# Moving the l2 norms, the convolution tails and the down-weight sums of a two-layer hybrid decoder

## The chip, the cores and the metric

The kernel runs on one core of a Trainium2 chip. The metric is the device time of one execution in microseconds. The time of the kernel before is the median of three runs, 2936.21 us (2934.1 to 2942.85).

## The reference

Two layers, each with a token-mixing and a channel-mixing sub-layer on a stream of 1024 tokens by 1024 features in float32. Mixing projects the normed stream into four head groups: A and B are gated linear recurrences, C is latent attention, D is a gated delta rule. The part of group D that the change touches is this:

```python
qkv = jax.nn.silu(causal_dwconv(jnp.concatenate([q, k, v], axis=-1), conv_w))   # width 4
qd = l2_norm(heads(qkv[..., :HD * DK_D], HD, DK_D)) * DK_D ** -0.5
kd = l2_norm(heads(qkv[..., HD * DK_D:2 * HD * DK_D], HD, DK_D))
vd = heads(qkv[..., 2 * HD * DK_D:], HD, DV_D)
```

Channel mixing is a gated MLP with D_FF = 2816 and a causal convolution of width 3 on the gate:

```python
gate = causal_dwconv(h @ w_gate, conv_w)
return (jax.nn.gelu(gate, approximate=True) * (h @ w_up)) @ w_down
```

## The kernel before, in words

Products of the projections and of the FFN are exact to about float32: each operand is split into a rounded part (hi, a cast on ScalarE, L197) and a rest (lo, a subtraction on GpSimd or VectorE, L198), and three matmuls (L209, `mm3`) replace one. The code gives a program order. A compile-time scheduler places each instruction in the queue of its engine by that order and by when it takes the operands to be ready, so a queue can hold instructions out of program order; each engine and the DMA queue of SP then work strictly in the order of their queue. `order`, `after` and `issue_after` (`behind` in `ffn1`) add edges that hold an instruction behind another one of the same engine.

**Mixing** (`mixing`, L1068 on) runs `proj_d`, `group_d`, two token-major projections (`tm_copy`), a gate, `proj_c`, `proj_a`, `proj_b`, two gates. One projection tile (`proj_fm`) is a 512 KB weight load through SP into one of two "wst" buffers, a cast on ScalarE, a subtraction on GpSimd, and 48 matmuls of 128x512. In `proj_d` (L809 on) six tiles q, k, v follow each other; each is convolved on VectorE (L825, L827), passed through a silu (L830, L831), and for the first four the squares (L834) are summed over a head by two matmuls with a block matrix of ones (L215), then Ln, Exp and a product on VectorE (L839 to L841) give the norm. All of this stands in the program behind its own tile and ahead of the next tile's projection. Tiles "t" (NT1 = 5 buffers) hold raw values, squares and most other temporaries; tiles "d" (ND = 11) hold q, k, v and group D's matrices.

**Sums of weights.** The FFN uses a Strassen-like scheme: of each pair of tiles seven products take the place of eight. Four of the seven need sums of weight blocks. `down_sums` (L1538) is a generator of 14 steps per layer: 10 pairs of the down weights (to a DRAM tensor `td`) and 4 tiles of the gate/up weights (to `te`). A step loads two tiles of 512 KB (L1550), makes four subtractions on GpSimd (L1555) and stores both tiles (L1562). `next(self.sums)` runs one step at each of 14 places in `mixing`: six in `proj_d`, two after the token-major copies, three in `proj_c`, two in `proj_a`, one of two in `proj_b`.

**FFN1** (`ffn1`, L1239) works through `seq`: 28 early products of the tiles f = 0 to 3 (operands partly from `te`), then seven products per f for f = 4 to 21. `prep(j)` makes the weight operand of product j: loads, sums (`operand_b`, L1223, GpSimd), split. It is called NLA = 7 products ahead; eight "wr" buffers hold operands. From f = 4 on the split of products 0 and 2 is on GpSimd, that of the other five on VectorE. `conv` (L1324) puts the two halves' boundary columns in place (L1329, L1334, GpSimd copies of 128x2), multiplies (L1335 ScalarE, L1337 VectorE twice), and applies the GELU (L1338). `store` (L1340) writes gated tiles and their sums to DRAM through SP. FFN2 (`Back`, `ffn2`) reads `td`.

Of the kernel before, what the change touches and what calls it, by code (L numbers as in the profile page):

```python
# [8 lines left out]
F32 = mybir.dt.float32  # L9
# [14 lines left out]
EPS = 1e-6  # L24
# [104 lines left out]
class Body:  # L129
# [447 lines left out]
    def proj_a(self, l, hT):  # L577
# [27 lines left out]
        for i in range(2):  # L605
            T = self.pt()
            self.proj_fm(l, hT, (AF0 + i, lambda n, p: nc.scalar.activation(
                out=T[:, n * 512:(n + 1) * 512], in_=p, func=AF.Tanh, scale=0.5)))
            next(self.sums, None)
            k = self.pt()  # L610
# [24 lines left out]
    def proj_b(self, l, hT, misc):  # L635
        nc = self.nc
        pp = self.pp
        q = self.pt()
        k = self.pt()
        for m, t in ((BQ, q), (BK, k)):  # L640
            self.proj_fm(l, hT, (m, self.copy_half(t)))
            next(self.sums, None)
        wgk = self.t("p1", "wgk", 1, [16, 128])
        nc.sync.dma_start(out=wgk, in_=self.I["wgk"][l])
        bg = pp[:, PP_BGK:PP_BGK + 1]
        f = self.pt()
        m = self.pt()
        for n in range(2):
            sl = slice(n * 512, (n + 1) * 512)
            p = self.ps([128, 512])  # L650
            self.mm(p, wgk, misc[0:16, sl])
            nc.scalar.activation(out=f[:, sl], in_=p, func=AF.Abs, bias=bg)
            nc.vector.tensor_scalar(out=m[:, sl], in0=p, scalar1=bg, scalar2=0.0, op0=ALU.add, op1=ALU.min)

        nc.scalar.activation(out=f, in_=f, func=AF.Tanh, scale=0.5)
        nc.scalar.activation(out=f, in_=f, func=AF.Ln, scale=0.5, bias=self.bias[0.5])
        nc.vector.tensor_tensor(out=m, in0=m, in1=f, op=ALU.add)
        self.cumsum(f, m)
        return self.spill("B", [q, k, f])


    def proj_c(self, l, hT, misc):
# [3 lines left out]
        for m in (CKV, CQ0, CQ1):  # L666
            t = self.t("k", "ckv", 1) if m == CKV else self.pt()
            self.proj_fm(l, hT, (m, self.copy_half(t)))
            next(self.sums, None)
            ts.append(t)  # L670
# [138 lines left out]
    def proj_d(self, l, hT, misc):  # L809
# [4 lines left out]
        for h in range(2):  # L814
            nc.gpsimd.memset(ones[64 * h:64 * h + 64, 64 * h:64 * h + 64], 1.0)
        fm = []
        for m in range(6):
            raw = self.pt()
            first = [(MISC, self.copy_half(misc))] if m == 0 else []
            self.proj_fm(l, hT, *first, (DQ0 + m, self.copy_half(raw)))  # L820
            next(self.sums)

# [9 lines left out]
            if m < 4:  # L832
                sq = self.pt()
                nc.scalar.activation(out=sq, in_=c, func=AF.Square)  # L834
                for n in range(2):
                    sl = slice(n * 512, (n + 1) * 512)
                    p = self.ps([128, 512])
                    self.mm(p, ones, sq[:, sl])
                    nc.scalar.activation(out=sq[:, sl], in_=p, func=AF.Ln, bias=self.bias[EPS * 4])  # L839
                nc.scalar.activation(out=sq, in_=sq, func=AF.Exp, scale=-0.5)  # L840
                nc.vector.scalar_tensor_tensor(out=c, in0=c, scalar=0.125 if m < 2 else 1.0, in1=sq, op0=ALU.mult, op1=ALU.mult)  # L841
            fm.append(c)
# [225 lines left out]
    def mixing(self, l, hT, x_src, x_dst):  # L1068
# [4 lines left out]
        misc = self.t("p1", "misc", 1)  # L1073
        self.td, self.sums = self.down_sums(l)
        dx = self.proj_d(l, hT, misc)
        od = self.group_d(l, *dx)
        av = self.spill("Av", self.tm_copy(l, TAI, hT))
        next(self.sums)
        bv = self.spill("Bv", self.tm_copy(l, TBV, hT))
        next(self.sums)  # L1080
        aG = self.gate(l, TAG, hT, self.rbh[:, RB_A:RB_A + 64], False)
# [156 lines left out]

    def ffn1(self, l, h, td, te):  # L1239

# [69 lines left out]
        def prep(j):  # L1310
# [5 lines left out]
            else:  # L1316
                if f not in B:
                    fetch(f)
                src = self.operand_b(i, *B[f])
            w = self.t(*(("w", "wr", 4) if j < 4 or j % 2 else ("f1" if j % 8 < 4 else "f0", "wr", 2)), [128, 2, 512], F32R)  # L1320
            self.split(w[:, 0, :], w[:, 1, :], src, nc.vector if j >= n_early and i not in (0, 2) else None)
            W[f, i] = w.rearrange("p e (k f) -> p e k f", f=128)

        def conv(f, n):  # L1324
# [3 lines left out]
            if n:  # L1328
                nc.gpsimd.tensor_copy(out=x[:, 0:2], in_=ends[f] if f < NE else z[f, 0][:, 512:514])  # L1329
            else:  # L1330
                nc.gpsimd.memset(x[:, 0:2], 0.0)
                if f < NE:
                    ends[f] = tails[:, 2 * f:2 * f + 2]
                    nc.gpsimd.tensor_copy(out=ends[f], in_=x[:, 512:514])  # L1334
            nc.scalar.activation(out=c, in_=x[:, 2:514], func=AF.Copy, scale=w(2))  # L1335
# [4 lines left out]
        def store(f):  # L1340

            p, e = divmod(f, 2)
            out = lambda i, x: nc.sync.dma_start(out=gd[7 * p + i], in_=x)
            if p >= NP:
# [30 lines left out]
        tails = self.t("f0", "tails", 1, [128, 2 * NE])  # L1375
        pa, pc, xs = {}, {}, {}
        for j, (f, i) in enumerate(seq):
            if j + NLA < len(seq):
                with behind("s2") if 1 < j < 7 else nullcontext():
                    prep(j + NLA)  # L1380
# [37 lines left out]
            elif i == 6:  # L1418
                add(xs[f, 1], xs[f, 1])
                nc.vector.tensor_tensor(out=g[f, 0], in0=g[f, 0], in1=xs[f, 1], op=ALU.mult)  # L1420
                store(f)
            if (f, i) == (NF - 1, 1):

                back = Back(self, l, gd, td)
                for _ in range(NU):
                    back.prep()
# [106 lines left out]

    def ffn(self, l, h, td, x_src, x_dst, last):
        gd, back = self.ffn1(l, h, *td)
        return self.ffn2(l, back, x_src, x_dst, last)

    def down_sums(self, l):  # L1538


        nc = self.nc
        td = self.dp.tile([NP, 128, 4, 512], F32, tag=self.nm("td"), name=self.nm("td"))
        te = self.dp.tile([NE, 128, 4, 512], F32, tag=self.nm("te"), name=self.nm("te"))

        def steps():
            for p in range(NP + NE):
                w = [self.t("p1", "d", ND) for _ in range(2)]
                for e in range(2):
                    src = self.I["wdn"][l, 2 * p + e] if p < NP else self.I["wgu"][l, p - NP, e].rearrange("p a b -> p (a b)")
                    nc.sync.dma_start(out=w[e], in_=src)  # L1550
                (b11, b12), (b21, b22) = ((x[:, 0:512], x[:, 512:1024]) for x in w)
                if p >= NP:

                    b12, b21 = b21, b12
# [3 lines left out]
                sub(b22, b22, b11)  # L1558
                sub(b21, b21, b22)
                for e in range(2):  # L1560
                    o = td[p] if p < NP else te[p - NP]
                    nc.sync.dma_start(out=o[:, 2 * e:2 * e + 2, :].rearrange("p a b -> p (a b)"), in_=w[e])  # L1562
                yield

        return (td, te), steps()

# [38 lines left out]
    def run(self):  # L1605
# [3 lines left out]
        for l in range(DEPTH):  # L1609
# [4 lines left out]
            dst = self.out if last else self.x2  # L1614
            hT = self.ffn(l, h, self.td, self.x1, dst, last)
            src = dst
# [51 lines left out]

NE, NLA, TRS = 4, 7, (1, 4)

# [32 lines left out]
```

## Time and profile before

| what | before |
|---|---|
| median of three runs | 2936.21 us |
| the profiled execution's own time | 2936.43 us |
| its span, first to last instruction | 2934.6 us |
| TensorE matmul busy | 2736.2 us (93%) |
| VectorE, ScalarE, GpSimd busy | 1838.8, 1328.4, 1187.8 us |
| mean granted TensorE clock | 0.974 |
| DMA | 386 MB, mean 132 GB/s |

The busy line says how much of the span an engine worked. Windows cut the span into stretches, and a stretch in which TensorE is busy for all of its 40 us at full clock can only get faster with less matmul work. Waits say which instruction of another engine or DMA ended an idle stretch. In a timeline a line gives start, duration, engine, line, operation, the tiles written and read, the shape, the number of merged instructions, and in brackets the idle time before and what ended it. SPq is the queue of SP, whose duration of a DMA line includes waiting inside a merged group.

### The profile page before, as it was taken

How to read it: one execution, taken by the hardware profiler on the slowest of the kernel's cores; microseconds unless marked ns; L12 is line 12 of the kernel's file. 1: busy time of each engine (PE TensorE's matmuls, PEld its weight loads, DVE VectorE, ACT ScalarE, POOL GpSimd, SP SyncE). 2: the span in 40 equal slices, each digit the busy share in tenths (PEclk: the TensorE clock that was granted, in tenths of full speed). 3: DMA queues.
4: the chain of work that ended last, by engine and by line, in shares of the span. 5: the costliest groups of instructions: out<-in, count | busy, mean ns of one | idle time of the engine just before them, and what ended most of it. 6: DMA issues, size and time to landing. Idle time of an engine off the chain costs nothing. (4 is left out here: it accounts for less than half of the span.)

```text
span 2934.6 us, 39974 instructions
## 1 busy us (share of the span) xinstructions
PE 2736.2 (93%) x14928; PEld 2224.1 (76%) x14928; DVE 1838.8 (63%) x2658; ACT 1328.4 (45%) x2422; POOL 1187.8 (40%) x1010
## 2 busy tenths in 40 slices
PE   7889888899989999999988998988999999999998
PEld 5688676677768888888767875866777778888887
DVE  4764433896477777665556643338965877776645
ACT  4423334645554444454445233346555544444543
POOL 4522453451675545300155225534526655443001
PEclk9989999999999999999999999999999999999999
DMA  5442553113443233376534315431234433333765
GB/s 188 138 109 66 177 196 113 55 51 111 138 129 112 100 108 108 105 271 195 186 131 149 106 60 197 180 106 58 67 107 144 140 108 101 100 101 104 259 193 194
DMA packets 162674, 386.02 MB, mean 132 GB/s; under 512 B 25488, under 2 KB 37040, under 8 KB 162480
## 3 DMA queue, kind: packets, MB, share of 16 engines
q1 hardware_dynamic: 162480, 383.47, 39.5%
q8 instruction: 117, 1.92, 0.3%
q14 instruction: 77, 0.63, 0.1%
HBM read 273.76 MB, written 109.64 MB: 131 GB/s over the span
## 5 line engine op out<-in xcount | busy, mean ns | idle before, releaser
L209 PE MATMUL pd<-h,wr 128*128 128x512 f32 x2608 | 662.6, 403 | 35.2 <-ACT wr L197 26.6
L209 PEld LDWEIGHTS pd<-h,wr 128*128 128x128 f32 x2608 | 491.1, 191 | 153.9 <-ACT wr L197 28.3
L198 POOL TENSOR_TENSOR wr<-wst,wr 128x512 fp32r<-128x512 f32 (+1 forms) x168 | 307.9, 1837 | 616.1 <-ACT wr L197 606.7
L197 ACT CAST wr<-wst 128x512 fp32r<-128x512 f32 (+1 forms) x260 | 196.6, 759 | 306.8 <-PE pd L209 202.0
L209 PE MATMUL pd<-wr,h 128*128 128x256 f32 x1920 | 249.3, 291 | 0.0
L209 PEld LDWEIGHTS pd<-wr,h 128*128 128x128 f32 x1920 | 242.0, 199 | 1.9 <-issue 0.5
L209 PE MATMUL pm<-h,wr 128*128 128x512 f32 x864 | 230.0, 392 | 1.7 <-DVE x L1399 1.6
L198 DVE TENSOR_TENSOR h<-st,h 128x1024 fp32r<-128x1024 f32 x120 | 152.3, 1272 | 120.9 <-ACT h L197 115.0
L209 PEld LDWEIGHTS pm<-h,wr 128*128 128x128 f32 x864 | 162.0, 188 | 39.3 <-DVE x L1399 2.4
L197 ACT CAST h<-st 128x1024 fp32r<-128x1024 f32 x120 | 125.6, 1049 | 145.8 <-PE pd L209 76.0
L209 PE MATMUL pd<-h 128*128 128x512 f32 x816 | 185.6, 389 | 0.0
L209 PE MATMUL pd<-wr,f 128*128 128x512 f32 x768 | 182.9, 395 | 0.0
L209 PEld LDWEIGHTS pd<-h 128*128 128x128 f32 x816 | 153.2, 188 | 31.8
L1337 DVE SCALAR_TENSOR_TENSOR g<-z,pp,g 128x512 f32<-128x512 f32 x176 | 164.2, 933 | 20.4 <-ACT g L1335 17.9
L209 PEld LDWEIGHTS pd<-wr,f 128*128 128x128 f32 x768 | 142.9, 188 | 32.0 <-ACT f L317 0.9
L209 PE MATMUL pm<-h 128*128 128x512 f32 x720 | 166.1, 391 | 0.7 <-DVE h L198 0.7
L1458 POOL TENSOR_TENSOR y<-y,gb 128x512 f32<-128x512 f32 x24 | 38.3, 1601 | 304.2 <-ACT fc L230 248.3
L198 DVE TENSOR_TENSOR wr<-wst,wr 128x512 fp32r<-128x512 f32 (+1 forms) x92 | 95.9, 1043 | 101.5 <-ACT wr L197 101.5
L209 PEld LDWEIGHTS pm<-h 128*128 128x128 f32 x720 | 135.5, 189 | 29.3 <-DVE h L198 1.1
L215 PE MATMUL pm<-g,g 128*128 128x128 f32 (+1 forms) x672 | 121.2, 329 | 30.1 <-issue 12.9
L215 PEld LDWEIGHTS pm<-g,g 128*128 128x128 f32 x672 | 99.3, 201 | 58.0 <-issue 30.3
L1555 POOL TENSOR_TENSOR d<-d,d 128x512 f32<-128x512 f32 x64 | 109.3, 1708 | 53.5 <-DMA d<-in_wgu_dram 48.3
(364 smaller groups left out, 5483.6 us busy)
## 6 DMA issues: line engine op xcount, KB each, us to landing
st<-gd SPq DMA_DIRECT2D x144, 256.0 KB, 3.0
gd<-g SPq DMA_DIRECT2D x88, 256.0 KB, 2.0
d<-in_wdn_dram SPq DMA_DIRECT2D x40, 512.0 KB, 5.4
td<-d SPq DMA_DIRECT2D x40, 512.0 KB, 2.7
st<-td SPq DMA_DIRECT2D x80, 256.0 KB, 3.6
ust<-in_wgu_dram SPq DMA_DIRECT2D x36, 512.0 KB, 3.7
wst<-in_wgu_dram SPq DMA_DIRECT2D x36, 512.0 KB, 3.6
st<-in_wdn_dram SPq DMA_DIRECT2D x68, 256.0 KB, 3.6
```

Of the source, the lines that this page charges most:

```text
L197: self.marks["hi"] = self.nc.scalar.copy(out=hi, in_=src)
L198: (eng or self.nc.gpsimd).tensor_tensor(out=lo, in0=src, in1=hi.bitcast(F32), op=ALU.subtract)
L209: mm = lambda x, y, **k: self.nc.tensor.matmul(out, lhsT=x, rhs=y, skip_group_check=onto, **k)
L215: self.nc.tensor.matmul(out, lhsT=lhsT, rhs=rhs, start=start, stop=stop)
L1337: nc.vector.scalar_tensor_tensor(out=c, in0=x[:, j:j + 512], scalar=w(j), in1=c, op0=ALU.mult, op1=ALU.add)
L1458: (dve if last and n else pool).tensor_tensor(out=y[t][:, c], in0=y[t][:, c], in1=g_post[:, c], op=ALU.mult)
L1555: sub = lambda o, x, y: nc.gpsimd.tensor_tensor(out=o, in0=x, in1=y, op=ALU.subtract)
```

## The change

- In `proj_d` the matmuls, Ln, Exp and product of the norm of tile m become a function that is called after the projection of tile m + 2.
- `down_sums` becomes `weight_sums`, made twice. In mixing only the four `te` steps are left, all taken from `proj_d`; the store of a step is issued at the next call. The eight later calls in mixing are removed.
- The ten `td` steps of a layer move into FFN1, each in three thirds (loads; subtractions; stores), one third after each product (f, 2) and (f, 6) with f >= 4, behind the last convolution copy on GpSimd and behind the last gated store on SP. They use two buffers "ds".
- To make room, FFN1 has six "wr" buffers in place of eight and NLA is 5 in place of 7. The same early products as before are held behind the split of s2.
- For f < 4 the convolution's boundary copies are on ScalarE in place of GpSimd.

```diff
 proj_d:
-        fm = []
+        fm, norms = [], []
         for m in range(6):
...
             self.proj_fm(l, hT, *first, (DQ0 + m, self.copy_half(raw)))
-            next(self.sums)
+            next(self.sums, None)
+
+            if m > 1:
+                norms.pop(0)()
...
             if m < 4:
                 sq = self.pt()
                 nc.scalar.activation(out=sq, in_=c, func=AF.Square)
-                for n in range(2):
...
+                def norm(c=c, m=m, sq=sq):
+                    for n in range(2):
+                        sl = slice(n * 512, (n + 1) * 512)
+                        p = self.ps([128, 512])
+                        self.mm(p, ones, sq[:, sl])
+                        nc.scalar.activation(out=sq[:, sl], in_=p, func=AF.Ln, bias=self.bias[EPS * 4])
+                    nc.scalar.activation(out=sq, in_=sq, func=AF.Exp, scale=-0.5)
+                    nc.vector.scalar_tensor_tensor(out=c, in0=c, scalar=0.125 if m < 2 else 1.0, in1=sq, op0=ALU.mult, op1=ALU.mult)
+                norms.append(norm)
 mixing (and the next(self.sums) of proj_a, proj_b, proj_c go):
-        self.td, self.sums = self.down_sums(l)
+        self.te, self.sums = self.weight_sums(
+            NE, lambda f, e: self.I["wgu"][l, f, e].rearrange("p a b -> p (a b)"), False, ("p1", "d", ND))
...
-        next(self.sums)
 ffn1, prep:
-            w = self.t(*(("w", "wr", 4) if j < 4 or j % 2 else ("f1" if j % 8 < 4 else "f0", "wr", 2)), [128, 2, 512], F32R)
+            w = self.t(*(("f0", "wr", 2) if j in (4, 5) or j > 5 and j % 3 == 2 else ("w", "wr", 4)), [128, 2, 512], F32R)
 ffn1, conv:
-                nc.gpsimd.tensor_copy(out=x[:, 0:2], in_=ends[f] if f < NE else z[f, 0][:, 512:514])
+                if f < NE:
+                    nc.scalar.copy(out=x[:, 0:2], in_=ends[f])
+                else:
+                    self.marks["conv"] = nc.gpsimd.tensor_copy(out=x[:, 0:2], in_=z[f, 0][:, 512:514])
...
-                    nc.gpsimd.tensor_copy(out=ends[f], in_=x[:, 512:514])
+                    nc.scalar.copy(out=ends[f], in_=x[:, 512:514])
 ffn1, the loop over seq:
+        td, td_steps = self.weight_sums(NP, lambda p, e: self.I["wdn"][l, 2 * p + e], True, ("f1", "ds", 2))
...
-                with behind("s2") if 1 < j < 7 else nullcontext():
+                with behind("s2") if 8 < j + NLA < 14 else nullcontext():
...
+            if f >= NE and i in (2, 6) and "conv" in self.marks:
+                with behind("conv"), behind("stored"):
+                    next(td_steps, None)
 weight_sums(n, src, cols, room), its steps:
+            for p in range(n):
+                w = [self.t(*room) for _ in range(2)]
                 for e in range(2):
+                    nc.sync.dma_start(out=w[e], in_=src(p, e))
+                if cols:
+                    yield
...
                 sub(b21, b21, b22)
+                yield
                 for e in range(2):
+                    nc.sync.dma_start(out=out[p][:, 2 * e:2 * e + 2, :].rearrange("p a b -> p (a b)"), in_=w[e])
+                if cols:
+                    yield
...
-NE, NLA, TRS = 4, 7, (1, 4)
+NE, NLA, TRS = 4, 5, (1, 4)
```

## Rows read from the trace of the kernel before

**Rows 1.** The profile page, part 1: busy time of each engine.
```profile
PE 2736.2 (93%) x14928; PEld 2224.1 (76%) x14928; DVE 1838.8 (63%) x2658; ACT 1328.4 (45%) x2422; POOL 1187.8 (40%) x1010
```

**Rows 2.** Windows of 40 us: length, busy PE, PEld, DVE, ACT, POOL, clock, DMA.
```profile
40.00:80.00 40.00, 35.37 (x143) 27.47 (x142) 18.65 (x10) 12.77 (x15) 21.33 (x12) 0.91 0.41 144
...
360.00:400.00 40.00, 23.49 (x88) 18.39 (x89) 17.03 (x14) 12.85 (x14) 23.18 (x16) 0.75 0.77 274
...
840.00:880.00 40.00, 28.93 (x106) 22.29 (x105) 30.32 (x39) 23.95 (x46) 34.88 (x19) 0.83 0.31 92
...
1000.00:1040.00 40.00, 40.00 (x176) 32.72 (x175) 29.54 (x35) 17.73 (x31) 18.95 (x16) 1.00 0.32 105
```

**Rows 3.** Waits of PE over the whole span: us in total, times, longest.
```profile
PE pd L209 <- ACT wr L197: 26.6, 2, 13.4
PE pm L215 <- ACT t L834: 23.0, 8, 4.6
...
PE pd L209 <- POOL wr L198: 14.5, 5, 6.8
```

**Rows 4.** Waits of PE, 40 to 165 us (first layer) and 1480 to 1640 us (second).
```profile
PE pm L215 <- ACT t L834: 12.4, 4, 4.6
...
PE pm L215 <- ACT t L834: 10.6, 4, 3.7
```

**Rows 5.** Timeline of PE around the first norm, first layer.
```profile
65.21 3.78 PE L215 MATMUL pm<-t,ones 128*128 128x512 f32 x4 [4.63 <-ACT t L834]
68.01 14.20 PE L209 MATMUL pd<-h,wr 128*128 128x512 f32 x57
```

**Rows 6.** Timeline of SPq and PE, 334 to 392 us, first layer.
```profile
334.21 9.24 SPq L1562 DMA_DIRECT2D td<-d  x4
...
358.31 0.80 SPq L1562 DMA_DIRECT2D te<-d  x2
...
362.97 0.50 SPq L192 DMA_DIRECT2D wst<-in_wfm_dram  x1
...
371.60 2.08 PE L209 MATMUL pd<-h,wr 128*128 128x512 f32 x4 [13.21 <-ACT wr L197]
...
375.74 13.16 PE L209 MATMUL pd<-h,wr 128*128 128x512 f32 x48 [2.06 <-POOL wr L198]
...
391.75 32.07 PE L209 MATMUL pd<-h,wr 128*128 128x512 f32 x140 [2.85 <-POOL wr L198]
```

**Rows 7.** Timeline at the start of FFN1, first layer; last line second layer.
```profile
843.16 10.82 POOL L1334 COPY tails<-z 128x2 f32<-128x2 f32 x1 [4.18 <-DVE z L1399]
...
853.94 7.56 POOL L198 TENSOR_TENSOR wr<-wst,wr 128x512 fp32r<-128x512 f32 x3
...
858.18 1.22 PE L209 MATMUL pd<-s2h,wr 128*128 128x512 f32 x2 [6.84 <-POOL wr L198]
...
2303.20 4.81 POOL L198 TENSOR_TENSOR wr<-wst,wr 128x512 fp32r<-128x512 f32 x3 [2.08 <-ACT wr L197]
```

**Rows 8.** Timeline of DVE and POOL in steady FFN1, 1012 to 1016 us.
```profile
1012.01 1.30 POOL L198 TENSOR_TENSOR wr<-wst,wr 128x512 fp32r<-128x512 f32 x1 [4.17 <-ACT wr L197]
1012.62 1.23 DVE L1417 TENSOR_TENSOR g<-g,x 128x512 f32<-128x512 f32 x1
1013.38 1.61 POOL L1223 TENSOR_TENSOR wst<-wst 128x512 f32<-128x512 f32 x1
1013.77 1.77 DVE L1420 TENSOR_TENSOR g<-g,x 128x512 f32<-128x512 f32 x1
```

**Rows 9.** Group of POOL in FFN1, 921 to 1191 us; DVE back to back.
```profile
L198 POOL TENSOR_TENSOR wr<-wst,wr 128x512 fp32r<-128x512 f32 x28 | 36.3, 1298 | 133.9 <-ACT wr L197 133.9
...
840.02 1.88 DVE L198 TENSOR_TENSOR s2l<-s,s2h 128x512 fp32r<-128x512 f32 x3
```

**Rows 10.** The moved work: GpSimd subtractions by line (ns min/median/max), loads of the page.
```profile
L1555 POOL TENSOR_TENSOR d<-d,d x64: 1265/1558/3164, 39.3 to 1861.3; 128x512 f32<-128x512 f32 x64
...
d<-in_wdn_dram SPq DMA_DIRECT2D x40, 512.0 KB, 5.4
```

More of the change, by code (lines that the diff above doesn't have):

```diff
@@ L608, in proj_a @@
                 out=T[:, n * 512:(n + 1) * 512], in_=p, func=AF.Tanh, scale=0.5)))
-            next(self.sums, None)
             k = self.pt()
@@ L641, in proj_b @@
             self.proj_fm(l, hT, (m, self.copy_half(t)))
-            next(self.sums, None)
         wgk = self.t("p1", "wgk", 1, [16, 128])
@@ L668, in proj_c @@
             self.proj_fm(l, hT, (m, self.copy_half(t)))
-            next(self.sums, None)
             ts.append(t)
@@ L834, in proj_d @@
                 nc.scalar.activation(out=sq, in_=c, func=AF.Square)
-                for n in range(2):
[L836 to L841, printed above, removed]
+                def norm(c=c, m=m, sq=sq):
[7 more added lines that the diff above has]
+                norms.append(norm)
             fm.append(c)
@@ L1077, in mixing @@
         av = self.spill("Av", self.tm_copy(l, TAI, hT))
-        next(self.sums)
         bv = self.spill("Bv", self.tm_copy(l, TBV, hT))
-        next(self.sums)
         aG = self.gate(l, TAG, hT, self.rbh[:, RB_A:RB_A + 64], False)
@@ L1237, in order, with ffn1 @@
             mybir.DependencyClass.NoSync, mybir.DependencyReason.DATA), reason="order")
-    def ffn1(self, l, h, td, te):
+    def ffn1(self, l, h, te):
         nc = self.nc
@@ L1342, in store, with out @@
             p, e = divmod(f, 2)
-            out = lambda i, x: nc.sync.dma_start(out=gd[7 * p + i], in_=x)
+            def out(i, x):
+                self.marks["stored"] = nc.sync.dma_start(out=gd[7 * p + i], in_=x)
             if p >= NP:
@@ L1532, in ffn2, with ffn, weight_sums @@
         return hT
-    def ffn(self, l, h, td, x_src, x_dst, last):
-        gd, back = self.ffn1(l, h, *td)
+    def ffn(self, l, h, te, x_src, x_dst, last):
+        gd, back = self.ffn1(l, h, te)
         return self.ffn2(l, back, x_src, x_dst, last)
-    def down_sums(self, l):
+    def weight_sums(self, n, src, cols, room):
         nc = self.nc
-        td = self.dp.tile([NP, 128, 4, 512], F32, tag=self.nm("td"), name=self.nm("td"))
-        te = self.dp.tile([NE, 128, 4, 512], F32, tag=self.nm("te"), name=self.nm("te"))
+        out = self.dp.tile([n, 128, 4, 512], F32, tag=self.nm("ts"), name=self.nm("ts"))
         def steps():
-            for p in range(NP + NE):
-                w = [self.t("p1", "d", ND) for _ in range(2)]
+            for p in range(n):
+                w = [self.t(*room) for _ in range(2)]
                 for e in range(2):
-                    src = self.I["wdn"][l, 2 * p + e] if p < NP else self.I["wgu"][l, p - NP, e].rearrange("p a b -> p (a b)")
-                    nc.sync.dma_start(out=w[e], in_=src)
+                    nc.sync.dma_start(out=w[e], in_=src(p, e))
+                if cols:
+                    yield
                 (b11, b12), (b21, b22) = ((x[:, 0:512], x[:, 512:1024]) for x in w)
-                if p >= NP:
+                if not cols:
                     b12, b21 = b21, b12
@@ L1559, in steps @@
                 sub(b21, b21, b22)
+                yield
                 for e in range(2):
[L1561 to L1565, printed above, removed]
+                    nc.sync.dma_start(out=out[p][:, 2 * e:2 * e + 2, :].rearrange("p a b -> p (a b)"), in_=w[e])
+                if cols:
+                    yield
+        return out, steps()
     def layer_params(self, l):
@@ L1614, in run @@
             dst = self.out if last else self.x2
-            hT = self.ffn(l, h, self.td, self.x1, dst, last)
+            hT = self.ffn(l, h, self.te, self.x1, dst, last)
             src = dst
```

## The prediction

> **What bounds the kernel now.** I read the busy line first: TensorE works for 2736 of 2934.6 us, so some 198 us of idle time and whatever the clock takes are all that this change can give [rows 1]. The windows say where that idle time lies. [...] In the stretches of the norms, at the end of `proj_c` and at the start of FFN1 it is busy for 35.4, 23.5 and 28.9 us, and the granted clock is 0.91, 0.75 and 0.83 [rows 2]. The waits of TensorE then name three causes, one for each of these stretches: a cast that came late (26.6 us in 2 waits, one in each layer), the squares of the norms (23.0 us in 8 waits, four tiles in two layers) and a split on GpSimd (14.5 us, of which one wait has 6.8) [rows 3]. Each is touched by one part of the change. The sum is made against the profiled execution's own 2936.4 us, which is 0.2 us above the median.
>
> **Norms two tiles later.** Before, the two matmuls of a norm stand in TensorE's queue in the middle of the next projection and wait for convolution, silu and square: 12.4 us in the first layer, 10.6 in the second [rows 4]. Two projection tiles later the squares are some 20 us old (48 matmuls at 40.00/176 = 0.227 us are 10.9 us a tile [rows 2]), so these waits go. The clock goes with them: behind the first wait the pair of matmuls took 3.78 us and the next 57 took 14.20, which is 0.249 each [rows 5] against 0.227; at a granted 0.91 a window of 40 us loses at most 3.6 us [rows 2], and the stage is over two windows long. I put 4 us on the clock in the first layer and 2 in the second, where the waits are shorter. What comes in their place: four norms' Ln, Exp and product queue ahead of the next silu on ScalarE and VectorE, but these were busy for 12.8 and 18.7 of 40 us there [rows 2]. The squares hold their "t" buffer for two tiles longer; five buffers hold raw 3, square 2, square 1, square 0 and raw 2 at the fullest, so a raw copy may wait for a norm's product. The last norm comes after the last projection, as late as group D can take it. I keep 4 us of new waits (0 to 15) in the two layers together. Term: -(12.4 + 10.6) - 6 + 4 = **-25**, bounds -10 and -32.
>
> **Sums out of mixing.** At 334 us SP stands for 9.2 us on four `td` stores that wait for GpSimd's subtractions; the `te` stores behind them are not issued until 358.3; only at 363.0 comes the load of the next projection's weights, and TensorE waits 13.2 us for its cast and 2.1 for its split [rows 6]; 2.85 us fall to the split after. The second layer repeats the cast's wait (26.6 us in two [rows 3]). The matmuls after the wait ran at 2.08/4 = 0.52 and 13.16/48 = 0.274 us [rows 6], which is 1.2 + 2.3 = 3.5 us more than at 0.227. So 21.7 us a layer hang on this queue. In the new order the four `te` steps sit in `proj_d`, where six `td` steps sat, with their stores one call later, so that SP has less to wait for; from there on SP and GpSimd carry no sums. But SP still holds the spills and the rotary table's store, which wait for VectorE, ahead of or beside these loads. I take back 15.5 us of the 21.7 in each layer: **-31**, bounds -8 and -43. The two steps after the token-major copies are costed at nothing: the large waits of rows 3 lie elsewhere.
>
> **Start of FFN1.** In the first layer a GpSimd copy of 128x2 took 10.8 us while VectorE worked without a pause; three splits queued behind it, and TensorE waited 6.8 us for the first; in the second layer the same splits got through in 4.8 us with no such copy in front [rows 7]. On ScalarE the eight copies are in front of an activation that needs the same tile, so they hold up nothing more. But the next GpSimd instruction is a split that reads SBUF as the copy does, and VectorE's run lasts as long. Also the lead of the operands falls from seven to five products. Term **-4** in the first layer, 0 in the second; bounds -10 and +8. [...]
>
> **The sums in FFN1.** Per layer 40 subtractions of at least 1.27 us and 20 loads and 20 stores of 512 KB, a load landing in 5.4 us [rows 10], in 30 thirds over some 15 tiles f. A tile f is 84 matmuls, 19.1 us at 0.227. Rows 8 show what the subtractions meet: the VectorE product started at 1012.62 and ended at 1013.85, just behind GpSimd's split that ended at 1013.31; the GpSimd sum then ended 1.14 us after that product. Instructions with two SBUF operands on VectorE and those of GpSimd go one after the other. Per tile VectorE has 13 of these (five splits, four convolution steps, two gated products, two sums for the store) at 1.88/3 = 0.63 us, GpSimd six of 1.30 [rows 9]: 8.2 + 7.8 = 16.0 us. The change adds 40/15 x 1.27 = 3.4: 19.4 of 19.1 us. So it is full. A lag of 0.3 us a tile is 4.5 us in 15 tiles, and operands are five products, 13.6 us, ahead. Each engine alone has room: VectorE is busy for 29.5 and GpSimd for 19.0 of 40 us [rows 2], and GpSimd sits 133.9 of 270 us ahead of its splits waiting for casts that wait for a free buffer [rows 9]. The cover is this lead: if it is gone, every microsecond by which a step outlasts it is TensorE's. Behind the waits that are added there are queued, on GpSimd, the splits of products 0 and 2 and the sums of the next tile, for which TensorE waits; on SP, the next gate/up loads and the gated stores. A load goes out when the fourth product of the tile before is split, six products (16.4 us) before its cast, so with a landing of 5.4 us SP may stand for 11 us. I take **+2** a layer, **+4** in all, bounds 0 and +20. FFN2 reads `td` only behind 22 products of its own; that costs nothing.
>
> **Sum.** 2936.4 - 25 - 31 - 4 + 4 = **2880 us**.
>
> **Rivals.**
> 1. *GpSimd's queue becomes FFN1's bound, slower.* A step's four subtractions, each taking turns with a VectorE instruction, last 4 x (1.27 + 0.63) = 7.6 us; where they directly follow their load by one product, 2.6 us of waiting for it come on top (5.4 - 2.8). If the splits behind them then have a lead of only GpSimd's own pause (4.2 us [rows 8]) rather than five products, a step costs 3.4 to 6 us. There are 20 steps; from 60/20 = 3.0 us a step on the gain is eaten. At 4 us it is 80 us: 2876 + 80 = **2956**. For it: 19.4 of 19.1 us. Against it: the 133.9 us of pauses and the lead. Chance 0.09. [...]
> 2. *SP finds another wait.* The table's store or a spill takes the place of the `td` stores, ahead of the same weight load. Then only a quarter of the second term comes: 2880 + 23 = **2903**. For it: SP serves strictly in order and the table's store is issued right behind the `te` stores. Against it: the load of the table itself is late because of the `td` stores. Chance 0.15.
> 3. *The norms wait anyway*, because buffers or ScalarE hold up the raw copies, so that the change does not do there what it says: the first term is -5 and the time **2900**. Against it: the low load of both engines. Chance 0.08. Together with rival 2: 2923, counted with rival 2.
>
> **How the numbers follow.** The forecast has 0.68. The range goes from the first two terms and the third at their large ends (2880 - 7 - 12 - 6 = 2855, less 7 for the clock behind waits that were not listed: 2848) to rivals 2 and 3 together, 2923; outside lie rival 1 and an unlucky order, under 2 in 10. About 0.3% (9 us) is what a measurement of this kernel can tell from no change. Faster by more than that: forecast and rivals 2 and 3 (0.91) less 0.05 for terms that all come out at their small ends, 0.86; within it 0.06, with a little of rival 1; slower 0.08.
>
> **What would show it.** Right: no wait for the squares in `proj_d`, and the last tile there done some 15 us earlier; no wait of over 5 us for a cast after `proj_c`, and no window there under a clock of 0.9; steady FFN1 still at 39.5 or more of 40 us busy, with GpSimd at some 26 in place of 19. Wrong: a wait of TensorE for `wr` on GpSimd or VectorE in steady FFN1, its windows below 39, or the weight load after `proj_c` issued late again behind another store. Waits of group D's chain that grow by what the norms gave back would say that the first term was hidden.

## The result and the profile after

The changed kernel takes 2916.31 us (median of four runs, 2914.06 to 2921.0) against 2935.47 for the kernel before beside it: ratio 0.9927, 95% interval 0.9911 to 0.9944. It is faster by 19 us where the forecast said 55. The profiled execution took 2916.28 us, its span is 2914.5.

The busy line of the page of the changed kernel answers to [rows 1]:

```profile
PE 2748.4 (94%) x14928; PEld 2230.1 (77%) x14928; DVE 1874.2 (64%) x2658; ACT 1329.0 (46%) x2442; POOL 1194.9 (41%) x994
```

The windows of the changed kernel, for the stretches of [rows 2] (length, busy PE, PEld, DVE, ACT, POOL, clock, DMA share, GB/s). The start of FFN1 comes some 22 us earlier in it (its first product on `s2` starts at 823.0 us, before at 844.8), so 818 to 858 us stands for 840 to 880:

```profile
40.00:80.00 40.00, 40.00 (x174) 32.46 (x173) 19.54 (x11) 11.91 (x15) 28.72 (x16) 1.00 0.48 172
360.00:400.00 40.00, 40.00 (x180) 32.28 (x179) 12.29 (x11) 14.74 (x19) 11.94 (x7) 1.00 0.35 125
818.00:858.00 40.00, 31.70 (x114) 24.63 (x113) 34.50 (x40) 24.33 (x49) 27.91 (x13) 0.83 0.29 79
1000.00:1040.00 40.00, 37.83 (x163) 30.25 (x162) 30.30 (x32) 16.91 (x30) 25.55 (x20) 1.00 0.47 161
```

The first two gaps of before are closed at full clock. The third is not: at the start of FFN1 TensorE is busy for 31.7 us where it was 28.9, and the clock is still 0.83. The window that was full now has 2.2 us of gaps and 163 matmuls instead of 176: a stretch that had no idle time got some. TensorE's waits over the whole span, beside [rows 3]:

```profile
PE pm L209 <- ACT x L1410: 22.8, 30, 1.9
...
PE pd L209 <- POOL wr L198: 8.6, 3, 4.1
...
PE pm L215 <- DVE du L875: 4.7, 2, 4.0
...
PE pm L998 <- DVE C L899: 4.0, 2, 2.0
```

The first is FFN1's: TensorE waits until ScalarE has copied a product out of its PSUM tile. The last two are group D's. The first and the last are new causes. (L998 of the changed kernel is L995 of the one before, L875 is L872.)

Where the time went, by the starts of the same instructions in each trace: change of each stage's length against before, both layers together, in us. D's projections end with the transposes of `misc`, group D with its last store of `od`, the other projections with the last token-major product; FFN1 runs from the first to the last convolution. Columns are the runs told of below; e15 and e4 are the kernel of before with parts of the change.

| stage | changed | e1 | e5 | e9 | e12 | e14 | e4 | e15 |
|---|---|---|---|---|---|---|---|---|
| D's projections | -33.0 | -32.5 | -12.2 | -32.5 | -32.4 | -33.0 | -28.8 | -28.4 |
| group D | +23.4 | +19.3 | -4.8 | +1.6 | +19.4 | +1.2 | +34.7 | +20.2 |
| other projections | -45.5 | -45.5 | -42.8 | -45.5 | -45.3 | -42.8 | +6.0 | +5.0 |
| attention to FFN1 | +4.6 | +5.6 | +2.3 | +3.3 | -0.3 | -0.6 | -0.2 | +2.4 |
| FFN1 | +31.2 | +1.3 | +30.8 | +33.9 | +17.1 | +14.1 | +1.7 | +5.8 |
| FFN2 | -0.9 | -1.3 | -0.9 | -1.1 | -0.8 | -1.3 | 0.0 | -1.4 |

So 78 us were won in the projections, 23 of them given back in group D and 5 up to FFN1, and 31 lost in FFN1. Each column is one execution. In e3, whose engines turned out to run the same instructions in the same order as the changed kernel's, these three are +17.4, +0.2 and +32.8: so 6 us in group D and all of the 5 up to FFN1 are what two executions can differ by. The experiments ask what took the time in group D and in FFN1. All medians are of four runs (ten for e15); the kernel before ran at 2934.6 to 2936.5 us beside them.

### The profile page after: what moved, and what is told of

Read it like the earlier page. It is cut to its first block, busy times and chain, and to the rows that moved or that the text cites. A ratio compares the mean times of both kernels' runs of the same rounds, so it can differ in the third digit from the quotient of the medians.

```text
span 2914.5 us, 39982 instructions
## 1 busy us (share of the span) xinstructions
PE 2748.4 (94%) x14928; PEld 2230.1 (77%) x14928; DVE 1874.2 (64%) x2658; ACT 1329.0 (46%) x2442; POOL 1194.9 (41%) x994
## 3 DMA queue, kind: packets, MB, share of 16 engines
q1 hardware_dynamic: 162480, 383.47, 39.3%
## 5 line engine op out<-in xcount | busy, mean ns | idle before, releaser
L209 PE MATMUL pd<-h,wr 128*128 128x512 f32 x2608 | 655.2, 401 | 0.4 <-POOL wr L198 0.4
L198 POOL TENSOR_TENSOR wr<-wst,wr 128x512 fp32r<-128x512 f32 (+1 forms) x168 | 341.6, 2036 | 506.8 <-ACT wr L197 502.4
L1342 DVE SCALAR_TENSOR_TENSOR g<-z,pp,g 128x512 f32<-128x512 f32 x176 | 214.7, 1220 | 102.2 <-ACT g L1340 87.6
L209 PEld LDWEIGHTS pd<-h 128*128 128x128 f32 x816 | 153.2, 188 | 31.7
L198 DVE TENSOR_TENSOR wr<-wst,wr 128x512 fp32r<-128x512 f32 (+1 forms) x92 | 103.4, 1124 | 74.0 <-ACT wr L197 74.0
L209 PE MATMUL pm<-hs,wr 128*128 128x512 f32 x528 | 132.1, 398 | 17.1 <-ACT x L1410 16.9
```

The source lines that it names most:

```text
L198: (eng or self.nc.gpsimd).tensor_tensor(out=lo, in0=src, in1=hi.bitcast(F32), op=ALU.subtract)
L209: mm = lambda x, y, **k: self.nc.tensor.matmul(out, lhsT=x, rhs=y, skip_group_check=onto, **k)
L1342: nc.vector.scalar_tensor_tensor(out=c, in0=x[:, j:j + 512], scalar=w(j), in1=c, op0=ALU.mult, op1=ALU.add)
```

## The experiments

### FFN1: what the moved subtractions cost

**e1, no subtractions in FFN1.**

```diff
-                sub(b11, b12, b11)
-                sub(b12, b22, b12)
-                sub(b22, b22, b11)
-                sub(b21, b21, b22)
+                if not cols:
+                    ...
```

> The changed kernel without the four subtractions of each down-weight step in FFN1; the steps' loads, stores and the single order of everything else stay (td then holds the plain weights, so the output is wrong by them). Theory, that GpSimd's subtractions hold up VectorE and through it the copies out of PSUM on ScalarE: FFN1's steady windows come back from 37-39.8 to 40.00 us of 40 on TensorE, both layers lose some 33 us, time 2884 us (2876 to 2892). Rival, that the steps' loads and stores (SP's queue, the DMA engines) hold up the gate and up weights: nothing to win, 2912 to 2920 us.

2880.05 us, ratio 0.9802 (0.9783 to 0.9821). FFN1 is back to the length of before (+1.3), with the loads, the stores, six operand buffers and a lead of five products all in place. The rival falls, and the shorter lead alone costs next to nothing. Its window:

```profile
1000.00:1040.00 40.00, 40.00 (x175) 32.60 (x174) 28.06 (x34) 17.86 (x31) 20.45 (x18) 1.00 0.44 151
```

**e2, constants written in place of the subtractions.**

```diff
-                sub(b11, b12, b11)
-                ...
+                for x in (b11, b12, b22, b21):
+                    for v in (1.0, 2.0, 3.0):
+                        nc.gpsimd.memset(x, v)
```

> The changed kernel with each of the four subtractions replaced by three writes of a constant over the same 128x512 operand (0.53 us each in the trace of the changed kernel, 12 of them 6.4 us against 6.2 for the four subtractions): GpSimd is as busy, but reads nothing from SBUF. Theory, that it is the reading of SBUF beside VectorE that costs: 2890 us (2880 to 2900), TensorE's windows at 39.5 or more. Rival, that GpSimd's queue is the bound (the weights that it prepares come late): 2910 to 2920, with TensorE's waits on ScalarE's copies unchanged at some 20 us over the span.

2892.38 us (0.9847, 0.9832 to 0.9861), as forecast; FFN1 +12.3. TensorE's seven windows from 920 to 1200 us are at 38.6 to 40.00, two of them below the 39.5 expected. GpSimd is as busy as in the changed kernel (193.0 us against 195.9 from 920 to 1200 us):

```profile
1000.00:1040.00 40.00, 40.00 (x175) 32.60 (x175) 29.24 (x33) 17.84 (x31) 26.85 (x34) 1.00 0.43 152
```

So 19 of the 31 us go with the reading, 11 with the time taken, and 1 stays without either. What GpSimd does to VectorE is in the groups of VectorE's two gated products, 920 to 1200 us, first of the changed kernel, then of e1, then the first of the two in e2 (busy, mean ns of one, idle before):

```profile
L1424 DVE TENSOR_TENSOR g<-g,x 128x512 f32<-128x512 f32 x14 | 21.6, 1541 | 0.0
...
L1427 DVE TENSOR_TENSOR g<-g,x 128x512 f32<-128x512 f32 x13 | 16.5, 1270 | 0.0
```

```profile
L1424 DVE TENSOR_TENSOR g<-g,x 128x512 f32<-128x512 f32 x15 | 12.4, 825 | 0.0
...
L1427 DVE TENSOR_TENSOR g<-g,x 128x512 f32<-128x512 f32 x15 | 10.2, 679 | 0.0
```

```profile
L1424 DVE TENSOR_TENSOR g<-g,x 128x512 f32<-128x512 f32 x14 | 19.4, 1386 | 0.0
```

And beside GpSimd's writes alone, in e2's timeline:

```profile
945.74 3.79 POOL L1575 MEMSET ds<- 128x512 f32 x8
946.27 0.68 DVE L1427 TENSOR_TENSOR g<-g,x 128x512 f32<-128x512 f32 x1
```

Such an instruction takes 0.68 us alone or beside a write, and up to 1.78 where it meets a GpSimd instruction of that size that reads. From 920 to 1200 us of e2 all 18 products and splits of VectorE that overlapped writes only took 0.67 to 0.69. In the changed kernel 11 of the 14 of L1424 took 1.77 or 1.78, in e1 2 of 15, in e2 9 of 14. Only 3 of the 11 overlap a moved subtraction; the other 8, and all 9 of e2, overlap GpSimd's own splits and sums, which meet this product more often when GpSimd has more to do. Of all of VectorE's 128x512 instructions with two tensor operands in this stretch, 98 of 218 took over 0.8 us in the changed kernel, 78 of 227 in e2, 66 of 233 in e1 and 64 of 230 before. In the kernel before, in the same stretch, all 64 of VectorE's 128x512 instructions with both operands in SBUF that overlapped a split or a sum of GpSimd took over 0.8 us, and the 43 with one operand in PSUM, which overlapped one too, 0.68 to 0.69.

**e3 and e6, the copy out of PSUM ahead of the convolution.** Products (f, 0), (f, 1), (f, 3) and (f, 4) use one PSUM tile, and ScalarE's copy of one must be done before the next starts; between (f, 1) and (f, 3), and between (f, 3) and (f, 4), there is one product, 2.7 us. In the changed kernel (timeline):

```profile
1138.09 1.77 DVE L1427 TENSOR_TENSOR g<-g,x 128x512 f32<-128x512 f32 x1
...
1140.38 0.68 DVE L1406 TENSOR_TENSOR z<-pd,x 128x512 f32<-128x512 f32 x1
...
1141.10 0.72 ACT L1340 ACTIVATE g<-z,pp 128x512 f32<-128x512 f32 x1 [5.17 <-DVE z L1406]
...
1141.72 0.56 ACT L1410 COPY x<-pm 128x512 f32<-128x512 f32 x1
...
1142.34 3.03 PE L209 MATMUL pm<-hs,wr 128*128 128x512 f32 x12 [1.61 <-ACT x L1410]
```

VectorE is late with z, ScalarE stands 5.17 us in front of the convolution's first step, the copy is behind it, TensorE waits 1.61 us.

```diff
-                conv(f, 0)
+                if f < NE:
+                    conv(f, 0)
...
-                nc.scalar.copy(out=x, in_=p)
+                ev = nc.scalar.copy(out=x, in_=p)
+                if i == 1 and f >= NE:
+                    conv(f, 0, ev)
```

e3 has this without `ev`; in e6 `self.order(ev, ...)` holds the convolution's first step behind the copy.

> The changed kernel with the convolution of a tile's first token half issued after the copy of the (f, 1) product out of PSUM instead of before it, for f from 4 on. Theory, that TensorE waits because this copy stands in ScalarE's queue behind a GELU that waits for VectorE: the wait of TensorE on the copies (22.8 us over the span) falls below 8 us, FFN1's windows come to 39 or more, time 2892 us (2882 to 2902). Rival, that VectorE as a whole does not keep up beside GpSimd's subtractions: TensorE's wait moves to VectorE's results or to another buffer, time 2908 to 2920.

2913.14 us (0.9919, 0.9900 to 0.9938). The scheduler gave every engine the same order as before the edit, so this is the changed kernel again: it tells nothing of the theory, but how far two executions differ. e6 forces the order:

> The changed kernel with the copy of the (f, 1) product out of PSUM held ahead of the convolution of the tile's first half on ScalarE by an order dependence, for f from 4 on; the earlier attempt only moved the call, and ScalarE's order stayed as it was. Theory of ScalarE's queue: TensorE's wait on the copies falls from 23-25 us below 8, FFN1's windows to 39 or more of 40, time 2892 us (2882 to 2902). Rival, that VectorE as a whole is late beside GpSimd's reads: the wait goes to another of VectorE's results or to the copy of (f, 3), time 2905 to 2918.

2910.87 us (0.991, 0.989 to 0.9929), the same within the measurement; the rival holds. The waits are half as many and last longer:

```profile
PE pm L209 <- ACT x L1412: 22.6, 16, 3.6
```

They also moved, as the rival said, to the copy of (f, 3): in the changed kernel 16.9 of the 22.8 us are in front of the products (f, 3) and 6.0 in front of (f, 4), in e6 0.5 and 22.1. ScalarE's order is only where VectorE's delay comes out.

**e12, the same subtractions on VectorE.**

```diff
+                eng = nc.vector if cols else nc.gpsimd
-                sub = lambda o, x, y: nc.gpsimd.tensor_tensor(out=o, in0=x, in1=y, op=ALU.subtract)
+                sub = lambda o, x, y: eng.tensor_tensor(out=o, in0=x, in1=y, op=ALU.subtract)
```

> The changed kernel with the four subtractions of each FFN1 step on VectorE instead of GpSimd. Uncontended, VectorE takes 0.68 us for a subtraction of this shape where GpSimd takes 1.56, and GpSimd's own reads go. Theory, that FFN1 loses by the two engines reading SBUF at once and not by VectorE's amount of work: VectorE rises by some 5.7 us of 40 to 34-35, TensorE's windows to 39.3 or more, time 2893 us (2885 to 2904). Rival, that VectorE's total is the limit: windows of 38 or less, VectorE above 34 of 40, time 2912 to 2935.

2896.66 us (0.9869, 0.9853 to 0.9885), 20 us under the changed kernel, of which 14 are in FFN1 (table): the busier engine does the work, and the kernel is the better for it. The time is as forecast; TensorE's windows from 920 to 1200 us, at 38.4 to 39.8, are mostly below the 39.3 expected.

```profile
1000.00:1040.00 40.00, 39.21 (x169) 31.39 (x168) 32.04 (x39) 17.11 (x31) 22.22 (x17) 1.00 0.43 151
```

VectorE's busy time rises by 1.7 us against the changed kernel's window, not by 5.7, since its other instructions shorten: from 920 to 1200 us 61 of 260 took over 0.8 us.

### The norms and group D

**e4, the norms' deferral alone**, on the kernel of before: `norm` as in the change, and

```diff
             next(self.sums)
+            if m > 1:
+                norms.pop(0)()
```

> The kernel of before with the norms two tiles later and nothing else of the change. Theory, that group D gives back what the projections win, because its dependent chain waits for ScalarE and VectorE, which now carry the norms' last part beside it, and because its matmuls run at the low level of the clock after each wait: projections of D end 19 us earlier in layer 0 and some 14 earlier in layer 1, the end of group D only 1 to 6 us earlier in each layer; time 2925 us (2920 to 2931). Rival, that the give-back comes from GpSimd's and VectorE's other order behind group D (the sums' steps are gone there in the full change): group D keeps the gain here and the time is 2902 us (2896 to 2910).

2950.1 us, ratio 1.005 (1.0034 to 1.0065): slower, outside both expectations. D's projections give 28.8 us, group D takes 34.7. Its start is late: from the transposes of `misc` to the first product on C 88.0 and 86.8 us pass in the two layers, 80.6 and 79.6 before. The first product that needs `du` waits up to 8.5 us there, 2.9 before; the last two norms stand ahead of `du` in ScalarE's and VectorE's queues. The granted clock, the expectation's second reason, was below 0.8 in four windows of 10 us of the first layer's group D (0.55, 0.74, 0.66 and 0.50), before in two (0.66 and 0.69).

**e5, the change without the deferral:**

```diff
-            if m > 1:
-                norms.pop(0)()
...
-                norms.append(norm)
+                norm()
```

> The changed kernel with the norms back in their tiles, all the rest of the change kept: the other half of the square to the run of the norms alone. Theory, that the norms' deferral costs about 13 us by itself, whatever the sums do (group D's chunks take 9 to 11 us longer in each layer): 2902 us (2895 to 2909), group D's chunks back at 110 us from the first L995 product to the last store. Rival, that without the sums' steps beside proj_d the deferral does pay, as the forecast had it: 2926 us or more (2920 to 2940).

2908.31 us (0.9903, 0.9882 to 0.9925), inside the theory's range, with the chunks at 111.1 and 111.0 us. By the medians the deferral costs 8 us within the change, 5 against e3; the intervals overlap, so a cost is not shown. What is shown is that it does not earn the 25 us of the forecast: it gives 20.8 in D's projections and takes 28.2 in group D (table; 22.2 with e3 for the changed kernel). The start of group D is no longer in the changed kernel than before (82.6 and 75.9 us). What is longer is the chunks. In the second one meeting occurs, in both layers alike (timeline of the changed kernel):

```profile
225.00 2.46 POOL L198 TENSOR_TENSOR wr<-wst,wr 128x1024 fp32r<-128x1024 f32 x1
225.17 2.84 DVE L410 SCALAR_TENSOR_TENSOR t<-gt,rbh 128x512 f32<-128x512 f32 x1
...
227.93 1.15 DVE L1066 SCALAR_TENSOR_TENSOR DS<-DS,ep,pm 64x64 f32<-64x64 f32 x4
...
229.11 0.78 DVE L899 TENSOR_TENSOR C<-pm,lm 32x64 f32<-32x64 f32 x3
229.47 0.41 PE L998 MATMUL pm<-d,C 32*32 32x32 f32 x4 [2.01 <-DVE C L899]
```

A weight's split on GpSimd starts 0.17 us before VectorE's gate operation, which takes 2.84 us instead of 0.69; the chain's next steps queue behind it, TensorE is idle for 2.0 us, and then works at a granted clock of 0.50 from 231.3 to 244.8 us, where it was 1.00 before and after:

```profile
220.00:230.00 10.00, 7.99 (x71) 7.26 (x70) 7.74 (x17) 3.30 (x6) 4.07 (x7) 1.00 0.14 28
230.00:240.00 10.00, 10.00 (x66) 6.17 (x65) 1.18 (x5) 2.10 (x7) 0.76 (x3) 0.56 0.37 131
240.00:250.00 10.00, 10.00 (x63) 8.96 (x61) 5.35 (x18) 1.75 (x4) 1.28 (x4) 0.76 0.04 13
```

**e7 and e9, that split on VectorE.** e7 took C's first weight, e9 the next one, which is the one that met the gate:

```diff
-                    ... self.weight(self.I["wfm"][l, m], [128, 8, 128])
+                    ... self.weight(self.I["wfm"][l, m], [128, 8, 128], eng=self.nc.vector if m == CQ0 else None)   # e9; e7 has CKV for CQ0
```

> The changed kernel with the split of one weight, the first of C's projections, on VectorE instead of GpSimd. In the changed kernel this split of 2.46 us began 0.17 us before VectorE's last gate operation in group D, which then took 2.84 us instead of 0.69; the chunk's C operation came late and TensorE, 2.0 us idle, ran at its low clock level for some 13 us after. Theory, that this one meeting is what lengthens group D's chunks: both waits on C go, group D's chunks return from 118-125 to 110 us in each layer, time 2899 us (2892 to 2906). Rival, that the chunks are slower for another reason (the token-major projections that filled TensorE are used up earlier): 2912 to 2920.

2912.08 us (0.9911, 0.9884 to 0.9938): the wrong split, the gate operation still took 2.84 us.

> The changed kernel with the split of the first of C's two query weights on VectorE. The run before took C's first weight off GpSimd, but the split that met VectorE's last gate operation was the next weight's: there the gate operation still took 2.84 us and TensorE still waited 2.0 us for C. Theory as before, that this one meeting lengthens group D's chunks: both 2.0 us waits on C go, the chunks (first L998 product to last store of od) return from 119-125 to 110-113 us in each layer, time 2899 us (2892 to 2907). Rival, that they are longer because the token-major projections are used up earlier: 2909 to 2918, chunks above 117 us.

2895.98 us (0.9856, 0.9837 to 0.9875), 20 us under the changed kernel for one instruction in each layer. The chunks last 113.3 and 110.9 us (changed 125.1 and 119.4, before 109.7 twice), and the same stretch of e9 shows why:

```profile
219.59 1.32 DVE L198 TENSOR_TENSOR wr<-wst,wr 128x1024 fp32r<-128x1024 f32 x1
...
222.67 0.41 PE L998 MATMUL pm<-d,C 32*32 32x32 f32 x4
...
224.57 0.68 DVE L410 SCALAR_TENSOR_TENSOR t<-gt,rbh 128x512 f32<-128x512 f32 x1
```

```profile
220.00:230.00 10.00, 9.91 (x97) 7.11 (x96) 6.23 (x17) 2.51 (x9) 2.51 (x3) 1.00 0.53 159
230.00:240.00 10.00, 9.98 (x80) 7.80 (x79) 4.96 (x18) 2.49 (x7) 1.40 (x6) 1.00 0.12 40
240.00:250.00 10.00, 10.00 (x91) 8.25 (x90) 3.30 (x8) 5.37 (x12) 2.33 (x7) 1.00 0.05 15
```

The intervals that end at the second and third stores of `od` take 15.8 and 19.4 us in both layers of the changed kernel, 13.7 and 13.9 in e9: 7.6 us a layer, 15 in both. The rest of the 20 is mostly in the first chunk, which in the first layer took 13.2 to 17.6 us in the runs that leave group D as the change has it, and is not this meeting's. In e9 VectorE's queue also has the gate operation behind the chain's steps (224.57) and not ahead of them, so the run takes away the meeting and that place together; a gate operation of 0.69 us ahead of the chain was not run. With the meeting gone the deferral pays: e9 is 12 us under e5.

**e15, the deferral and that split**, on the kernel of before:

```diff
 on e4
-                    ... self.weight(self.I["wfm"][l, m], [128, 8, 128])
+                    ... self.weight(self.I["wfm"][l, m], [128, 8, 128], eng=self.nc.vector if m == CQ0 else None)
```

> The kernel of before with the norms two tiles later, and C's first query weight split on VectorE. Theory, that the deferral lost its gain to the meeting of this split with VectorE's gate operation: group D's chunks, 121 us in the run of the norms alone, are back at 110 to 113 in each layer and the time is 2930 us (2923 to 2938), some 20 below the 2950 of the norms alone. Rival, that beside the sums' steps of this kernel the deferral costs by itself: 2942 to 2955.

2940.05 us (1.001, 0.9997 to 1.0022), between the two. The chunks are back at 113.0 and 110.9 us, as the theory said, but group D is still 20 us longer than before, mostly at its start (87.5 and 88.3 us), where the waits for `du` are, first before, then in e15:

```profile
PE pm L215 <- DVE du L872: 5.6, 2, 2.9
```

```profile
PE pm L215 <- DVE du L878: 17.0, 2, 8.5
```

So beside the sums as they stood before, six `td` steps in `proj_d` among them, the deferral earns nothing; beside the sums of the change it earns 12 us (e9 against e5).

### Better versions

**e8, e10, e16: some down-weight steps in the projections of A, B (and C)**, each step's stores issued at the next call, the rest in FFN1. e10 is e9 with this for four steps:

```diff
+        self.dsums = self.weight_sums(4, ..., 2, ("p1", "d", ND), 0, self.td)[1]
...
             self.proj_fm(l, hT, (AQ0 + i, evac))
+            next(self.dsums, None)
...
             self.proj_fm(l, hT, (m, self.copy_half(t)))     # proj_b
+            next(self.dsums, None)
```

> The changed kernel with nine of the ten down-weight steps moved from FFN1 into the projections of C, A and B, each step's stores issued with the next step's loads so that SP does not wait for subtractions just issued; the tenth step stays in FFN1. Theory, that those projections have the room (GpSimd 10-12 of 40 us, VectorE 8-19, TensorE at 40.00) and that the stall of before came from stores waiting in SP's queue: FFN1's windows near 40, the projections' windows stay at 40.00, time 2886 us (2878 to 2896). Rival, that the steps stall the projections again, by SP's queue or by GpSimd's splits coming late: windows of 36 to 39 at the end of C's projections, 2900 to 2925.

Nine steps: 2907.49 us (0.9895, 0.9868 to 0.9921). FFN1 is healed (+2.1), but the other projections keep only 24.6 of their 45.5 us; both readings are half right. TensorE waits there for GpSimd:

```profile
360.00:400.00 40.00, 34.70 (x145) 27.86 (x144) 11.26 (x9) 12.50 (x15) 28.95 (x20) 0.96 0.77 270
```

> The run with C's query weight on VectorE, and besides four of the ten down-weight steps in the projections of A and B, one to two projections; six stay in FFN1. Nine steps there made TensorE wait for GpSimd's splits (19.7 us over the span) and cost the projections about 10 us. Theory, that at one step to two splits GpSimd keeps up: no waits for wr there beyond 6 us, FFN1 wins 1.7 us a step, 13 us in both layers, against the run without it: 2886 us (2878 to 2898). Rival, that stores in SP's queue hold up the next weights at any density: 2895 to 2912.

Four steps: 2885.87 us (0.9828, 0.9814 to 0.9843), as forecast. e11 is the same on e5, with the norms in place:

> The run with the norms in place, with the same four down-weight steps in the projections of A and B. By additivity 2908 - 13 = 2895 us (2886 to 2904), group D's chunks at 111 us. Rival as in the run above: 2904 to 2918.

2896.51 us (0.9872, 0.9854 to 0.989), where additivity said 2895.

**e13, e14 and e16, both cures together.** e13 is e9 with e12's line, e14 is e10 with it for the six steps left in FFN1, and e16 has six steps in the projections and four in FFN1:

```diff
 e13, on e9
+                eng = nc.vector if cols else nc.gpsimd
 e14, on e10
+                eng = nc.vector if cols == 1 else nc.gpsimd
 e16, on e14
-        self.dsums = self.weight_sums(4, ...)[1]
+        self.dsums = self.weight_sums(6, ...)[1]
...
             self.proj_fm(l, hT, (AF0 + i, ...))             # proj_a
+            next(self.dsums, None)
```

> The changed kernel with C's first query weight split on VectorE and FFN1's subtractions on VectorE. Theory, that the two causes are independent: the gains against the changed kernel, 20 us each, add up to 2876 us (2870 to 2884). Rival, that they share something (the clock, or VectorE's backlog): 2886 to 2897.

2881.07 us (0.9813, 0.9798 to 0.9827): 35 us under the changed kernel where the sum would be 40. The two causes are nearly independent.

> The run with four down-weight steps in the projections of A and B, with the subtractions of the six steps in FFN1 on VectorE. Subtractions on VectorE won 20 us over 20 steps, 1 us a step: 12 steps, 2886 - 12 = 2874 us (2867 to 2881). Rival, that the six steps that are left cost so little that nothing is won: 2882 to 2888.

2875.56 us, ratio 0.9797 (0.9777 to 0.9817): the best, 61 us under the kernel before and 41 under the changed one.

> As the run with four steps in the projections and FFN1's subtractions on VectorE, with six steps in the projections of A and B and four in FFN1. Theory, that six still fit between the splits: two steps fewer in FFN1 at about 0.7 us each and two layers, 2871 us (2864 to 2880). Rival, that TensorE waits for GpSimd's splits in the projections again, as with nine: 2876 to 2890, waits for wr above 12 us over the span.

2886.11 us (0.9837, 0.9815 to 0.9859): worse than four steps, with other projections at -40.3 and attention to FFN1 at +7.3, though the waits for wr (9.5 us) stay below the rival's 12. Where its loss comes from was not followed further.

## Why the prediction was right or wrong

**Direction and range: right.** The kernel is faster, inside 2848 to 2923. The gain is a third of the forecast's. That it lies inside the range is partly luck: by the runs the four terms came to 0 to +8, -60, +1 and +30 us, so the second, twice its forecast, paid for the first and the last; none of these three lies inside its own bounds.

**Norms two tiles later (-25): the step that failed is the last one, that what the projections win reaches the end.** The waits for the squares are gone, and on the kernel of before (e4) D's projections won 28.8 us, the 29 of the working before its allowance of 4. Within the change it was 20.8 (changed against e5), because there the waits for the squares were already down from 23.0 to 13.4 us. But group D gave 28.2 back (22.2 by e3): net 0 to +8. The text said that the last norm comes "as late as group D can take it", named a growth of that chain's waits as the sign of a hidden term, and priced all new waits together at 4 us. What it did not see is that the scheduler's new order would set a split beside a gate operation: 15 us in two layers by the stores of `od`, 20 by the medians (e9), of which the two windows of layer 0 above lose up to 10 x (0.44 + 0.24) = 6.8 us to the clock. Rival 3 had the right sign against the term, but no wait of TensorE in `proj_d` shows the raw copies late.

**Sums out of mixing (-31): mechanism right, size too small.** With the norms in place (e5) the other projections won 42.8 us, the whole 21.7 a layer that hung on the queue, so no other SP wait took its place (rival 2 falls), and D's projections and group D won another 12.2 and 4.8. That the four `te` steps stand "where six `td` steps sat" had been given no time; it was worth that.

**Start of FFN1 (-4): about +1.** The 10.8 us copy and the wait of 6.84 us behind it are gone, but in each layer TensorE waits 4.1 us for a split, which in the second is new, and still 4.2 for `s2h`. FFN1 without the subtractions (e1) is 1.9 us shorter than before in the first layer and 3.2 longer in the second. The text read that the second layer has no such copy in front of its splits; it has the same copy there, which took 0.58 us beside a VectorE that also worked without a pause, so the rows do not tell when such a copy is held up.

**The sums in FFN1 (+4): the step that failed is the cover.** The working found the tile full, 19.4 us of instructions that take turns in 19.1, and the runs bear out that VectorE falls behind. It then let the lead of five products cover it. Operands were never late: between 905 and 1250 us every wait of TensorE is for the copy. What is late is VectorE's other work and, through ScalarE, the copies that free a PSUM tile; their lead is one product (2.7 us). Measured +30 us (changed against e1), 1.5 us a step, where the bounds were 0 and +20. Rival 1 had the engine right and the victim wrong: it made the split queue the bound, at 3 to 6 us a step.

## What to carry to other kernels

Here moving work into a full stretch cost by the shortest lead there, not by the longest: list every buffer that a late engine frees, with how many products of the bound engine lie between. Work on GpSimd that reads SBUF was paid on VectorE here (one gated product took 0.83 us on average without the subtractions, 1.54 with them), and the same subtraction was cheaper on the busier VectorE (e12). When a wait is removed ahead of a dependent chain, read the chain too: a new order can set two instructions side by side that met nobody before, and a single 2 us gap there came with 7.6 us more a layer.

## What the runs showed of the hardware that had not been expected

After one idle stretch of 2.0 us in group D the granted clock was 0.56 and 0.76 in the next two windows of 10 us, while in steady FFN1 thirty waits of up to 1.9 us left it at 1.00; with waits of up to 3.6 us there (e6) two windows of 40 us fell to 0.91 and 0.96. GpSimd's writes of constants, 128x512 in 0.53 us each, did not slow the 18 products and splits of VectorE that overlapped them alone (0.67 to 0.69 us, e2).
